# One core, two attention layers: where the norm weight and the gate enter the first one, and the size of one row sum

## The chip, the core and the metric

The kernel runs on one core of a Trainium2 chip. The core has five engines that run side by side, each with its own in-order queue: TensorE (PE in the profile; its weight loads stand apart as PEld), VectorE (DVE), ScalarE (ACT), GpSimd (POOL) and SyncE (SP), which here only issues DMAs. The metric is the device time of one execution in microseconds; a median over runs is compared with a median.

## What is computed

The reference is one inference step of a two-layer streaming encoder, in float32. 2048 new frames of one stream ("prompt") and 64 frames of a running stream ("sample", with 256 cached frames) go through both layers; width 1024, 4 heads of width 256. The layer that the change touches is the first one, differential attention:

```python
s = einsum('bqhmd,bkhmd->bhmqk', q, k) * DIFF_DH ** -0.5      # two maps m = 0, 1 per head
p = softmax(where(visible, s, NEG_INF))                        # block-causal mask, chunks of 64
w = p[:, :, 0] - lam * p[:, :, 1]                              # learned scalar lam
o = w @ v                                                      # 256 wide per head
o = rmsnorm(o, subln_w) * (1 - lam_init)                       # norm over the head's 256 values
o = o * silu(g)                                                # g: the gate, a projection of the input
y = x + o @ w_out
```

The second layer is stick-breaking attention (a running sum along each row in place of the softmax). A final RMSNorm follows, and the keys and values of both layers are outputs too.

## The kernel before

Everything is held transposed, with features on the 128 partitions and frames along the free axis. A float32 product is made of three matmuls: each operand is split into a rounded high half and a low rest (`split`, line 51 to 54: ScalarE copies the high half, VectorE or GpSimd subtracts), and `mm3` (lines 57 to 62) issues low x high, high x low and high x high.

The stages follow one another: the first layer's projections (`p_phase`, 0 to about 770 us in the profile), the first attention (`a_phase` with `layer == 0`, about 770 to 1314 us), the output projection (`o_phase`), the second layer's projections (`p_strassen`), the second attention (`a_phase` with `layer == 1`, about 2240 to 2735 us) and the last output projection with the final norm.

`do_g` in `p_phase` makes the gate: it evaluates silu in seven steps on VectorE and ScalarE and writes the result to a scratch tensor `gT` in HBM, from which the attention reads it back.

In `a_phase` the work of one head is cut into five query groups: one of the 64 sample frames (against 320 keys) and four of 512 prompt frames (against 512, 1024, 1536 and 2048 keys). A group has four rows of 128 queries. For a row, `diff_unit` makes two maps: per 512 keys TensorE fills a PSUM tile `s`, and VectorE moves it to SBUF and takes its maximum (line 727); ScalarE takes the exponential of each whole map (line 735); VectorE computes the weight of the second map (lines 738 and 739) and adds the second map, times that weight, to the first in one instruction as long as the row (line 742). Row lengths run from 128 to 2048 columns.

With four rows done, the group's product with the values runs key block by key block: `transposed` turns the four 128 x 128 pieces of a block into one PSUM tile `tp` (line 791), splits it into `wh` and `wl`, and `pv_block` adds six matmuls into the two PSUM tiles `o`. There are only two `o` tiles, so the next group's first product has to wait until both have been read.

`mixed` ends a group. It issues the load of the gate `g` (one buffer per width), reads both `o` tiles with ScalarE twice, once squared into `sq` (line 827) and once times the norm weight into `ot` (line 829, or 840 for the last group; one `ot` buffer per width), and GpSimd adds the squares up. `finish`, called one key block into the next group, sums the squares over the partitions by a matmul with ones (line 844), makes the norm factor, multiplies `ot` by it (line 859, by VectorE at line 857 for the last group) and by the gate (line 860), and stores `ot`.

The order in each queue is not the order of the program text alone: a planner (`schedule_with_timeline_sim=True`) orders the instructions at build time by its own estimate of when each can start, and places the semaphores. The generators interleave the stages: matmuls of the next row and row operations of the previous one are drawn in turn by their `yield` costs, and the rows run ahead of the products by `LEAD` units.

Of the kernel before, what the change touches and what calls it, by code (L numbers as in the profile page):

```python
# [8 lines left out]
F32 = mybir.dt.float32  # L9
# [3 lines left out]
AF = mybir.ActivationFunctionType  # L13
ALU = mybir.AluOpType
# [3 lines left out]
P = 128  # L18
# [10 lines left out]
LAM_INIT = 0.8 - 0.6 * math.exp(0.0)  # L29
# [65 lines left out]
def p_phase(tc, k, layer, xsrc, rs):  # L95
# [4 lines left out]
    nc = tc.nc  # L100
    with ExitStack() as es:
# [160 lines left out]
        def do_g(h, wt, ti, ps0=None):  # L262
            t0, w = TT[ti]
            for s in range(2):
                ps = ps0 if s == 0 and ps0 is not None else proj_t(wt, s * P, ti)
                e, o = work("t1" if s else "t2", bufs=1)[:, :w], work("o1" if s else "o2")[:, :w]
                nc.vector.scalar_tensor_tensor(o, ps, -0.5, rbc[ti], ALU.mult, ALU.mult)
                r = op.tile([P, 2, 256], F32R, tag="s2", name="r", bufs=2).rearrange("p a b -> p (a b)")
                r = r[:, :w].bitcast(F32)
                nc.scalar.activation(e, o, AF.Exp, scale=-1.0)  # L270
                nc.vector.tensor_scalar(e, e, 1.0, 1e37, ALU.add, ALU.min)
                nc.scalar.activation(r, e, AF.Ln)
                nc.scalar.activation(r, r, AF.Exp, scale=-1.0)
                nc.vector.tensor_tensor(e, e, r, ALU.mult)
                nc.vector.scalar_tensor_tensor(o, o, -1.0, r, ALU.mult, ALU.mult)
                nc.vector.scalar_tensor_tensor(o, e, -2.0, o, ALU.add, ALU.mult)
                r0 = h * HW + s * P
                nc.sync.dma_start(out=k.gT[layer][r0:r0 + P, t0:t0 + w], in_=o)
# [14 lines left out]
        with pool(tc, f"prep{layer}") as pk:  # L293
            first, stat = prep(order[0], pk)
            st = [stat]
# [333 lines left out]
def a_phase(tc, k, layer):  # L629
    nc = tc.nc  # L630
    ck, cv = k.ckT[layer], k.cv[layer]
    with ExitStack() as es:
# [12 lines left out]
        if layer == 0:  # L645
            wk = es.enter_context(pool(tc, f"aw{layer}", 1))
        psp = es.enter_context(pool(tc, f"aps{layer}", 2, space=PSUM))
        osc = None
        if layer == 0:
            osc = wk.tile([P, 2], F32, name="osc")  # L650
            nc.scalar.activation(osc, k.subln_w, AF.Copy, scale=-0.5 * (1.0 - LAM_INIT))

        def pair(pl, tag, shape, bufs=None):
            t = pl.tile([P, 2] + shape, F32R, tag=tag, name=tag, bufs=bufs)
# [57 lines left out]
        def diff_unit(row, j, nq, qt, chunks, diag, s15):  # L712

            nk = sum(w for _, w, _ in chunks)
            nch = len(chunks)
            qs = slice(j * P, j * P + nq)
            st = wk.tile([P, 16], F32, tag="st", name="st", bufs=16)[:nq]
            r2 = rbp.tile([P, 2052], F32, tag="rb", name="r2")
            sc = float(P) ** -0.5
            maps = (row, r2)  # L720

            def matmuls():
                for m in range(2):
                    for ci, (kt, w, wn) in enumerate(chunks):
                        ps = psp.tile([P, 512], F32, tag="s", name="s", bufs=3)
                        s_matmul(ps, nq, wn, qt, qs, kt, [m], diag if ci == nch - 1 else None, w)
                        nc.vector.tensor_scalar(maps[m][:nq, ci * 512:ci * 512 + w], ps[:nq, :w], 1.0, None,  # L727
                                                ALU.mult, ALU.max, accum_out=st[:, 4 * m + ci:4 * m + ci + 1])
                        yield w / 2048
                    mx = st[:, 4 * m:4 * m + nch]  # L730
                    nc.vector.tensor_scalar(mx, mx, -sc, None, ALU.mult, ALU.min, accum_out=st[:, 8 + m:9 + m])

            def rowops():
                for m in range(2):
                    nc.scalar.activation(maps[m][:nq, :nk], maps[m][:nq, :nk], AF.Exp, scale=sc,
                                         bias=st[:, 8 + m:9 + m], accum_out=st[:, 10 + 2 * m:11 + 2 * m])
                    yield nk / 4096
                nc.vector.reciprocal(st[:, 14:15], st[:, 12:13])
                nc.vector.scalar_tensor_tensor(st[:, 14:15], st[:, 14:15], k.nlam[:nq], st[:, 10:11],
                                               ALU.mult, ALU.mult)  # L740
                nc.scalar.activation(s15[:nq, j:j + 1], st[:, 10:11], AF.Square, scale=(EPS * HW) ** 0.5)
                nc.vector.scalar_tensor_tensor(row[:nq, :nk], r2[:nq, :nk], st[:, 14:15], row[:nq, :nk],
                                               ALU.mult, ALU.add)
                yield nk / 2048

            return matmuls(), rowops()

# [69 lines left out]
        def mixed(u):  # L817

            h, wq, nq, t0 = u.h, u.wq, u.nq, u.t0
            oa, ob = u.o  # L820
            g = (gp if wq == 512 else wk).tile([P, 2, wq], F32, tag=f"g{wq}", name="g")
            nc.sync.dma_start(out=g, in_=rows(k.gT[layer], h, t0, t0 + wq))
            ot = wk.tile([P, 2, wq], F32, tag=f"ot{wq}", name="ot")
            if layer == 0:
                sq = wk.tile([P, 2, wq], F32, tag=f"sq{wq}", name="sq")
                for e, o in ((0, oa), (1, ob)):
                    nc.scalar.activation(sq[:, e, :wq], o[:, :wq], AF.Square)
                    if not u.last:
                        nc.scalar.activation(ot[:, e, :wq], o[:, :wq], AF.Copy, scale=osc[:, e:e + 1])
                nj = len(u.rows)  # L830
                dg = wk.tile([P, wq], F32, tag=f"rm{wq}", name="dg")
                nc.gpsimd.tensor_tensor(dg[:nq].rearrange("p (j q) -> p j q", j=nj),
                                        k.idn[:nq, :nq].unsqueeze(1).to_broadcast([nq, nj, nq]),
                                        u.s15[:nq, :nj].unsqueeze(2).to_broadcast([nq, nj, nq]), ALU.mult)
                (nc.vector if u.last else nc.gpsimd).tensor_tensor(sq[:nq, 0, :wq], sq[:nq, 0, :wq], dg[:nq], ALU.add)
                (nc.vector if u.last else nc.gpsimd).tensor_tensor(sq[:, 0, :wq], sq[:, 0, :wq], sq[:, 1, :wq],
                                                                   ALU.add)
                if u.last:
                    for e, o in ((0, oa), (1, ob)):
                        nc.scalar.activation(ot[:, e, :wq], o[:, :wq], AF.Copy, scale=osc[:, e:e + 1])  # L840

                def finish():
                    ss = psp.tile([P, 512], F32, tag="t", name="ss", bufs=3)[:, :wq]
                    nc.tensor.matmul(ss, k.ones, sq[:, 0, :wq], start=True, stop=True)
                    r = wk.tile([P, wq], F32, tag=f"rs{wq}", name="rs")
                    m = wk.tile([P, wq], F32, tag=f"rm{wq}", name="rm")
                    t = sq[:, 1, :wq]
                    nc.scalar.activation(m, ss, AF.Copy, scale=1.0 / HW)
                    nc.scalar.activation(r, m, AF.Ln)
                    nc.scalar.activation(r, r, AF.Exp, scale=-0.5)  # L850
                    nc.scalar.activation(t, r, AF.Square)
                    nc.gpsimd.tensor_tensor(t, t, m, ALU.mult)
                    nc.vector.tensor_scalar(t, t, -3.0, None, ALU.add)
                    nc.gpsimd.tensor_tensor(r, t, r, ALU.mult)
                    for e in range(2):
                        if u.last:
                            nc.vector.tensor_tensor(ot[:, e, :wq], ot[:, e, :wq], r, ALU.mult)
                        else:
                            nc.gpsimd.tensor_tensor(ot[:, e, :wq], ot[:, e, :wq], r, ALU.mult)
                        nc.gpsimd.tensor_tensor(ot[:, e, :wq], ot[:, e, :wq], g[:, e, :wq], ALU.mult)  # L860
                    nc.sync.dma_start(out=rows(k.oT[layer], h, t0, t0 + wq), in_=ot[:, :, :wq])

                unfinished.append(finish)
            else:
                for e, o in ((0, oa), (1, ob)):
                    nc.vector.tensor_tensor(ot[:, e, :wq], o[:, :wq], g[:, e, :wq], ALU.mult)
                nc.sync.dma_start(out=rows(k.oT[layer], h, t0, t0 + wq), in_=ot[:, :, :wq])
# [217 lines left out]
def trunk(ctx: ExitStack, tc, xT, wqkg, wv, wo, small, ckT, cv, rope, masks, idn,  # L1085
          yT, kT, v):
    nc = tc.nc
    k = K()
# [43 lines left out]
    k.y1T = dp.tile([D, T], F32, name="y1T")  # L1132
    k.xop = [dp.tile([7, P, 4, PW], F32, name=f"xop{i}") for i in range(2)]
    k.xs = dp.tile([P, NC, NS], F32, name="xs")
    k.wnm = cp.tile([P, NC], F32, name="wnm")
    nc.vector.tensor_scalar(k.wnm, k.norm_w[:, 1], -0.5, None, ALU.mult)

# [91 lines left out]
```

## Time and profile before

| | before |
|---|---|
| median of 3 runs | 2928.25 us (2926.78 to 2929.58) |
| the profiled execution's own time | 2934.8 us |
| its span, first to last instruction | 2933.0 us |
| TensorE busy | 2809.2 us, 96% of the span |
| VectorE busy | 1905.4 us, 65% |
| ScalarE busy | 1444.3 us, 49% |
| GpSimd busy | 572.4 us, 20% |
| mean granted TensorE clock | 0.984 of full speed |

The profile is one execution, taken instruction by instruction. A busy share is an average over stages that are limited in different ways, so a change in one stage is read from that stage's windows, waits and timeline. A wait is put down to the instruction whose end released it last.

### The profile page before, as it was taken

What the parts mean: (1) busy time and instruction counts of PE and PEld (TensorE: products, weight loads), DVE (VectorE), ACT (ScalarE), POOL (GpSimd) and SP (SyncE); (2) the same over time, 40 slices, a digit from 0 to 9 for tenths busy, and PEclk for the clock granted to TensorE, in tenths of its full rate; (3) what the DMA queues carried; (4) which work ended last, traced back from release to release, by engine and by line L of the source; (5) the groups of instructions that cost most, each with busy time, mean ns of one, the idle gap of its engine ahead of it and who ended that gap; (6) DMA issues with size and microseconds to landing.
All of it is one profiled execution on the core that took longest, in us unless ns stands there. A gap on an engine that the chain in (4) does not pass through costs nothing.

```text
span 2933.0 us, 45474 instructions
## 1 busy us (share of the span) xinstructions
PE 2809.2 (96%) x16342; PEld 2446.4 (83%) x16342; DVE 1905.4 (65%) x3586; ACT 1444.3 (49%) x2763; POOL 572.4 (20%) x639
## 2 busy tenths in 40 slices
PE   8999999999899999989989999999997999999998
PEld 7888998988787777768777987899996788788788
DVE  7644514345378887854556688765686988877455
ACT  6512322313466666653234444543455877776433
POOL 1233233231233544443000000000000000000321
PEclk9999999999999999999999999999998999999999
DMA  5577456354715443336754677765727334523442
GB/s 175 166 195 189 138 156 179 132 147 128 269 62 185 139 137 121 115 101 210 248 178 154 223 238 244 253 201 166 241 97 239 137 123 156 175 76 104 162 143 98
DMA packets 365938, 484.01 MB, mean 165 GB/s; under 512 B 63504, under 2 KB 208144, under 8 KB 365712
## 3 DMA queue, kind: packets, MB, share of 16 engines
q1 hardware_dynamic: 350560, 466.67, 49.8%
q10 hardware_dynamic: 15152, 14.44, 1.5%
q8 instruction: 129, 2.11, 0.3%
q14 instruction: 97, 0.79, 0.1%
HBM read 273.10 MB, written 207.88 MB: 164 GB/s over the span
## 4 chain that ended last, share of the span: by engine, by line
PE 67%; DVE 15%; DMA 8%; ACT 6%; issue 3%; POOL 1%; SPq 0%; ACTq 0%; DVEq 0%; POOLq 0%
PE pj L58 13%; PE pj L62 13%; PE pj L61 13%; DVE rowA L775 4%; PE ps L58 3%; PE ps L62 3%; PE ps L61 3%; PE o L58 3%; PE o L62 3%; PE o L61 3%; PE tp L791 2%; DVE rowA L772 2%; PE s L58 2%; PE s L62 2%; PE s L61 2%
## 5 line engine op out<-in xcount | busy, mean ns | idle before, releaser
L58 PE MATMUL pj<-x,wop 128*128 128x272 f32 (+1 forms) x1008 | 330.7, 330 | 26.1 <-DVE x L54 21.0
L58 PE MATMUL pj<-hl,whi 128*128 128x512 f32 (+2 forms) x960 | 340.3, 355 | 3.2 <-ACT whi L53 3.2
L61 PE MATMUL pj<-hh,wlo 128*128 128x512 f32 (+2 forms) x960 | 338.9, 353 | 1.0 <-POOL wlo L54 1.0
L62 PE MATMUL pj<-hh,whi 128*128 128x512 f32 (+2 forms) x960 | 338.6, 353 | 0.0
L62 PE MATMUL pj<-x,wop 128*128 128x272 f32 (+1 forms) x1008 | 328.5, 327 | 0.0
L61 PE MATMUL pj<-x,wop 128*128 128x272 f32 (+1 forms) x1008 | 328.2, 326 | 0.0
L58 PE MATMUL s<-k,q 128*128 128x512 f32 (+3 forms) x656 | 266.5, 407 | 23.9 <-DVE rowA L727 6.9
L58 PE MATMUL o<-wl,v 128*128 128x512 f32 (+4 forms) x688 | 270.4, 393 | 15.6 <-DVE wl L54 9.4
L62 PE MATMUL o<-wh,v 128*128 128x512 f32 (+4 forms) x688 | 250.7, 365 | 0.0
L61 PE MATMUL o<-wh,v 128*128 128x512 f32 (+4 forms) x688 | 249.8, 363 | 0.0
L54 DVE TENSOR_TENSOR wl<-tp,wh 128x512 fp32r<-128x512 f32 (+5 forms) x344 | 195.1, 576 | 83.7 <-ACT wh L53 83.2
L53 ACT ACTIVATE s<-o 128x256 fp32r<-128x256 f32 (+2 forms) x212 | 84.2, 404 | 333.2 <-DMA kS<-s 127.0
L61 PE MATMUL s<-k,q 128*128 128x512 f32 (+3 forms) x656 | 241.2, 368 | 0.0
L62 PE MATMUL s<-k,q 128*128 128x512 f32 (+3 forms) x656 | 241.2, 368 | 0.0
L58 PEld LDWEIGHTS pj<-x,wop 128*128 128x128 f32 x1008 | 191.1, 190 | 52.9 <-DVE x L54 30.2
L58 PE MATMUL ps<-ol,wh 128*128 128x512 f32 (+2 forms) x640 | 227.3, 355 | 6.2 <-DVE ol L54 6.2
L756 POOL MEMSET z<- 128x1 f32 (+1 forms) x68 | 12.0, 177 | 1123.9 <-PE pj L62 777.3
L61 PE MATMUL ps<-oh,wl 128*128 128x512 f32 (+2 forms) x640 | 229.4, 358 | 0.0
L53 ACT ACTIVATE wh<-tp 128x512 fp32r<-128x512 f32 (+5 forms) x344 | 169.5, 507 | 119.8 <-PE tp L791 106.2
L62 PE MATMUL ps<-oh,wh 128*128 128x512 f32 (+2 forms) x640 | 227.1, 355 | 0.0
L58 PEld LDWEIGHTS pj<-hl,whi 128*128 128x128 f32 x960 | 182.0, 190 | 26.9 <-ACT whi L53 3.5
L61 PEld LDWEIGHTS pj<-x,wop 128*128 128x128 f32 x1008 | 191.9, 190 | 14.7 <-DVE wop L54 0.6
(231 smaller groups left out, 7354.3 us busy)
## 6 DMA issues: line engine op xcount, KB each, us to landing
wraw<-in_wqkg SPq DMA_DIRECT2D x144, 256.0 KB, 3.9
vS<-s SPq DMA_DIRECT2D x128, 256.0 KB, 3.4
v<-vS SPq DMA_DIRECT2D x64, 512.0 KB, 5.2
q<-qS SPq DMA_DIRECT2D x60, 512.0 KB, 6.0
k<-kS SPq DMA_DIRECT2D x60, 512.0 KB, 7.3
wraw<-in_wv SPq DMA_DIRECT2D x64, 256.0 KB, 3.5
qS<-s SPq DMA_DIRECT2D x128, 128.0 KB, 2.4
kS<-s SPq DMA_DIRECT2D x128, 128.0 KB, 2.4
```

What stands on the lines that cost most here:

```text
L53: nc.scalar.activation(hi, x, AF.Copy)
L54: lo_eng.tensor_tensor(lo, x, hi.bitcast(F32), ALU.subtract)
L58: first = nc.tensor.matmul(ps, lh, rl, start=start, stop=False, skip_group_check=True)
L61: nc.tensor.matmul(ps, ll, rh, start=False, stop=False, skip_group_check=True)
L62: nc.tensor.matmul(ps, lh, rh, start=False, stop=stop, skip_group_check=True)
L756: nc.gpsimd.memset(z[:nq, nk:nk + 1], 0.0)
L772: nc.vector.scalar_tensor_tensor(rr, zz, 0.0, rr, ALU.min, ALU.subtract)
L775: nc.vector.tensor_tensor_scan(rv, z[:nq, c1:c0:-1], rv, r[:nq, c1:c1 + 1] if done else 0.0, ALU.add, ALU.subtract)
L791: nc.tensor.transpose(tp[:kn, j * P:j * P + u.nq], u.rows[j][:u.nq, i * P:i * P + kn], k.idn[:u.nq, :u.nq])
```

## The change

Three edits. The norm weight times 0.5 x (1 - lambda_init), which ScalarE applied as it read `o`, becomes a per-partition factor `k.nosc` in the gate's second last step (its sign is folded in: the gate was multiplied by -1.0 there). The product of `o` with the gate, which GpSimd made at the very end of `finish`, is made by VectorE straight from PSUM in place of ScalarE's scaled copy. And the sum of the two maps (line 742) is issued in pieces of at most 1024 columns, with a yield after each.

```diff
-                nc.vector.scalar_tensor_tensor(o, o, -1.0, r, ALU.mult, ALU.mult)
+                nc.vector.scalar_tensor_tensor(o, o, -1.0 if layer else k.nosc[:, s:s + 1], r, ALU.mult, ALU.mult)
...
-        osc = None
-        if layer == 0:
-            osc = wk.tile([P, 2], F32, name="osc")
-            nc.scalar.activation(osc, k.subln_w, AF.Copy, scale=-0.5 * (1.0 - LAM_INIT))
...
-                nc.vector.scalar_tensor_tensor(row[:nq, :nk], r2[:nq, :nk], st[:, 14:15], row[:nq, :nk],
-                                               ALU.mult, ALU.add)
-                yield nk / 2048
+                for c0, c1 in pieces(nk):
+                    nc.vector.scalar_tensor_tensor(row[:nq, c0:c1], r2[:nq, c0:c1], st[:, 14:15], row[:nq, c0:c1],
+                                                   ALU.mult, ALU.add)
+                    yield (c1 - c0) / 2048
...
                     if not u.last:
-                        nc.scalar.activation(ot[:, e, :wq], o[:, :wq], AF.Copy, scale=osc[:, e:e + 1])
+                        nc.vector.tensor_tensor(ot[:, e, :wq], o[:, :wq], g[:, e, :wq], ALU.mult)
...
                 if u.last:
                     for e, o in ((0, oa), (1, ob)):
-                        nc.scalar.activation(ot[:, e, :wq], o[:, :wq], AF.Copy, scale=osc[:, e:e + 1])
+                        nc.vector.tensor_tensor(ot[:, e, :wq], o[:, :wq], g[:, e, :wq], ALU.mult)
...
-                        nc.gpsimd.tensor_tensor(ot[:, e, :wq], ot[:, e, :wq], g[:, e, :wq], ALU.mult)
...
+    k.nosc = cp.tile([P, 2], F32, name="nosc")
+    nc.vector.tensor_scalar(k.nosc, k.subln_w, 0.5 * (1.0 - LAM_INIT), None, ALU.mult)
```

`pieces(nk)` cuts 0 to nk into steps of 1024. It was there before, for the second layer.

## Rows read from the trace of the kernel before

**Rows 1.** The page's first part: busy time of an engine, share of the span, instructions.

```profile
PE 2809.2 (96%) x16342; PEld 2446.4 (83%) x16342; DVE 1905.4 (65%) x3586; ACT 1444.3 (49%) x2763; POOL 572.4 (20%) x639
```

**Rows 2.** Busy time by stretch of the span. Columns: the stretch in us, its length, busy us (and instructions) of PE, PEld, DVE, ACT and POOL, the granted TensorE clock, the DMA share and GB/s. The first stretch lies in the first layer's projections; the others in the first attention: most of it, the first 25 us of two heads, and the end.

```profile
250.00:500.00 250.00, 250.00 (x1495) 226.32 (x1494) 102.02 (x169) 67.57 (x150) 83.63 (x88) 1.00 0.58 161
...
803.00:1276.00 473.00, 457.22 (x2484) 370.08 (x2484) 380.74 (x1191) 298.01 (x603) 196.91 (x198) 1.00 0.37 123
...
950.00:975.00 25.00, 23.15 (x122) 18.40 (x121) 23.05 (x68) 17.77 (x29) 16.39 (x17) 1.00 0.27 89
...
1200.00:1225.00 25.00, 22.70 (x125) 18.04 (x124) 21.31 (x65) 17.37 (x35) 15.21 (x19) 1.00 0.28 88
...
1275.00:1300.00 25.00, 18.79 (x83) 14.86 (x84) 14.83 (x18) 14.79 (x28) 17.48 (x12) 0.80 0.33 104
```

**Rows 3.** What TensorE waited for in the first attention (803 to 1314 us): the waiting instruction, its releaser, us in total, times, the longest.

```profile
PE tp L791 <- DVE rowA L742: 8.0, 4, 4.1
PE s L58 <- DVE rowA L727: 5.2, 4, 2.7
PE o L58 <- DVE wl L54: 3.3, 2, 3.0
PE ss L844 <- DVE sq L836: 2.3, 1, 2.3
PE s L58 <- DMA k<-kS: 2.2, 1, 2.2
PE s L58 <- DVE r L727: 1.6, 1, 1.6
...
PE ss L844 <- POOL sq L836: 0.9, 2, 0.7
```

**Rows 4.** Single waits of TensorE in that stage, from its timeline. Columns: start, duration, engine, line, instruction, shape, count of like neighbours, and in brackets the idle time before it and its releaser.

```profile
882.00 0.55 PE L791 MATMUL tp<-idn,rowA 128*128 128x128 f32 x3 [1.14 <-DVE rowA L742]
...
892.72 0.55 PE L791 MATMUL tp<-idn,rowA 128*128 128x128 f32 x3 [1.41 <-DVE rowA L742]
...
963.71 0.50 PE L58 MATMUL s<-k,q 128*128 128x512 f32 x1 [1.74 <-DVE rowA L727]
...
1278.16 0.90 PE L791 MATMUL tp<-idn,rowA 128*128 128x128 f32 x3 [4.07 <-DVE rowA L742]
...
1282.11 0.80 PE L58 MATMUL o<-wl,v 128*128 128x512 f32 x1 [3.05 <-DVE wl L54]
```

**Rows 5.** The start of the kernel, from the timelines of TensorE and ScalarE: the first matmul, and ScalarE writing the fourth quarter of the weight tile `whi` that this matmul reads from.

```profile
5.66 0.77 PE L58 MATMUL pj<-wlo,hh 128*128 128x256 f32 x2 [5.66 <-ACT hh L150]
...
10.83 0.63 ACT L53 ACTIVATE whi<-wraw 128x512 fp32r<-128x512 f32 x1 [1.19 <-DMA wraw<-in_wv]
```

**Rows 6.** Groups of instructions by line and shape. Columns: line, engine, operation, tiles, out shape <- in shape, count, busy us, mean ns of one, idle time before them. Lines 829, 860 and 742 in the first attention, 772, 775 and 866 in the second.

```profile
L829 ACT ACTIVATE ot<-o,osc 128x512 f32<-128x512 f32 x30 | 19.9, 690 | 1.0 <-DMA oT<-ot 1.0
...
L860 POOL TENSOR_TENSOR ot<-ot,g 128x512 f32<-128x512 f32 x30 | 44.0, 1482 | 0.0
...
L742 DVE SCALAR_TENSOR_TENSOR rowA<-r,st,rowA 128x2048 f32<-128x2048 f32 x4 | 9.4, 2346 | 0.0
...
L772 DVE SCALAR_TENSOR_TENSOR rowA<-z,rowA 128x1024 f32<-128x1024 f32 x40 | 48.6, 1216 | 16.5 <-ACT rowA L771 16.3
...
L775 DVE TENSOR_TENSOR_SCAN rowA<-z,rowA 128x1024 f32<-128x1024 f32 x40 | 94.2, 2354 | 0.3
...
L866 DVE TENSOR_TENSOR ot<-o,g 128x512 f32<-128x512 f32 x32 | 21.2, 680 | 1.4 <-PE o L62 1.2
...
L866 DVE TENSOR_TENSOR ot<-o,g 128x64 f32<-128x64 f32 x8 | 1.4, 209 | 0.0
```

**Rows 7.** The end of the first attention, from the timelines of VectorE and ScalarE (same columns as rows 4).

```profile
1275.76 2.35 DVE L742 SCALAR_TENSOR_TENSOR rowA<-r,st,rowA 128x2048 f32<-128x2048 f32 x1
1278.03 3.43 DVE L54 TENSOR_TENSOR ol<-oraw,oh 128x512 fp32r<-128x512 f32 x2
1281.38 1.87 DVE L54 TENSOR_TENSOR wl<-tp,wh 128x512 fp32r<-128x512 f32 x3
...
1311.66 0.68 ACT L840 ACTIVATE ot<-o,osc 128x512 f32<-128x512 f32 x1
```

**Rows 8.** The start of the second head, from the timelines of GpSimd, VectorE and ScalarE.

```profile
960.27 3.22 POOL L860 TENSOR_TENSOR ot<-ot,g 128x512 f32<-128x512 f32 x3
...
960.93 2.11 DVE L742 SCALAR_TENSOR_TENSOR rowA<-r,st,rowA 128x1408 f32<-128x1408 f32 x1
...
955.84 1.07 ACT L827 ACTIVATE sq<-o 128x512 f32<-128x512 f32 x2
...
966.39 1.25 ACT L829 ACTIVATE ot<-o,osc 128x512 f32<-128x512 f32 x2
```

**Rows 9.** Waits that bear on the moved product: SyncE's queue in the first attention, and TensorE in the second (the same columns as rows 3).

```profile
SPq L861 <- POOL ot L860: 224.7, 18, 25.1
...
PE o L58 <- DVE ot L866: 4.8, 4, 1.8
```

**Rows 10.** The gate's step and an instruction of the same kind with a per-partition factor, both in the first projections (columns as rows 6), and the constant beside which the new one is made (min/median/max ns, first and last start in us).

```profile
L275 DVE SCALAR_TENSOR_TENSOR o<-o,r 128x512 f32<-128x512 f32 x24 | 17.5, 730 | 0.0
...
L151 DVE SCALAR_TENSOR_TENSOR hl<-x,vecs,hh 128x512 fp32r<-128x512 f32 x24 | 18.4, 772 | 9.3 <-ACT hh L150 9.3
...
L1136 DVE TENSOR_SCALAR wnm<-vecs x1: 173/173/173, 4.3 to 4.3; 128x8 f32<-128x8 f32 x1
```

## The prediction

> **What bounds the kernel now.** I read the page's busy times first: TensorE is busy for 96% of the span, VectorE for 65% [rows 1]. So the change can shorten the kernel only where TensorE waits. The windows come next, cut at the stage that the change touches: from 803 to 1276 us TensorE is busy 457.2 of 473.0 us and VectorE 380.7, or 80% [rows 2]. VectorE is the second fullest engine there, and in the first 25 us of the second head it is as busy as TensorE, 23.05 against 23.15 us. Third, the waits: those of TensorE that are listed come to 23.5 us, and all but 3.1 have VectorE as releaser [rows 3]. ScalarE releases none. This is the purse: the change cannot give much more than that, and a microsecond saved on ScalarE or GpSimd is worth something only through VectorE's queue.
>
> The timeline shows where those waits lie [rows 4]. Four are transposes that wait for a sum of the two maps (8.0 us with the one of 1.4 that is left of the total [rows 3]). The largest pair stands at the end of the stage: 4.07 us for the last sum, then 3.05 us for `wl`, and the granted clock of that stretch is 0.80 [rows 2], so matmuls after the pause also run longer. Others are matmuls of `s` whose PSUM tile VectorE has not emptied yet, because a long sum stands ahead in its queue.
>
> **Part 1, the weight folded into the gate.** 40 instructions of the first projections get a per-partition factor in place of a constant. A like instruction with such a factor takes 772 ns, the present one 730 [rows 10]; both means hold some that ran long. At worst 40 x 0.04 = 1.7 us more on VectorE, and what hides it is TensorE, busy 250.00 of 250.00 us there with VectorE at 102 [rows 2]. Cost 0; were that cover gone, 1.7. The constant is one more instruction like the 173 ns one at 4.3 us [rows 10]: 0, at most 0.2. The dropped `osc` was one short ScalarE instruction: 0.
>
> **Part 2, o times gate on VectorE.** ScalarE loses 40 copies, the 512-wide at 690 ns, GpSimd loses 40 products, the 512-wide at 1482 ns [rows 6]. VectorE gains 32 products of 680 ns and 8 of 209, priced by the same instruction in the second attention [rows 6]: 21.8 + 1.7 = 23.5 us, which takes its share of the stage from 80% to about 85%.
>
> What is queued behind the new instruction on VectorE are the emptying of `s`, the `wl` halves and the sums, all of which TensorE waits for. Its own waits could be three. *The gate*: its buffer is now free as soon as the product is made, a whole group ahead, and in the second attention, where the same load stands in front of the same product, VectorE idles 1.2 us for `o` and nothing for the gate [rows 6]: cost 0. *The `ot` buffer*: it is free when the previous group's store has read it. The store stands in SyncE's queue behind GpSimd's gate product, 224.7 us of waiting in 18 [rows 9]; it now follows the product before that one and goes 2 x 1.5 us sooner [rows 6]. Cost 0; if it is still late, VectorE and not ScalarE is held, and the 1.0 us that ScalarE waited [rows 6] is the bound. *Two readers of one `o` tile*: if ScalarE's square and VectorE's product had to take turns, that would be the present sequence on one engine, so no worse.
>
> *The release of `o`.* In the second head ScalarE squares at 955.84 but copies only at 966.39 [rows 8]: the `ot` buffer is held by a late `finish`, and the next group's products wait with it. TensorE fills the time with `s` matmuls, which is what crowds VectorE. The new order frees `o` some microseconds sooner. Against that, the second attention shows what the moved product can cost: TensorE waits 4.8 us in 4 places for it [rows 9], there behind scans of 2.35 us [rows 6]. Here the longest will be the pieces, 1.22. I take a loss of 1.0 us, between 0 (now, with ScalarE) and 4.8.
>
> *The start of each head*, where VectorE is full. Against: a 64-wide and a 512-wide pair, 0.4 + 1.2 us, come into a stretch with 1.95 us of VectorE left [rows 2]; half of it on the path in three heads is 2.4 us. For: the 1408-wide sum took 2.11 us while GpSimd made gate products, and TensorE waited 1.74 us behind it [rows 4, 8]; a like wait of 1.6 stands in the list [rows 3]. In two pieces, and with the gate product gone from GpSimd, each of these loses about 0.9: 1.8. And the ones-matmul waits 0.9 us for squares that stood behind gate products on GpSimd [rows 3]: 0.9. Net gain 0.3, between a loss of 4.4 and a gain of 4.4 (all the waits there).
>
> *The last group*: of the 2.3 us wait before its ones-matmul [rows 3], ScalarE's copy between the two squares (0.68) [rows 7] goes. Gain 0.4; if the planner puts both products ahead of the additions on VectorE, a loss of 1.0.
>
> **Part 3, the sum in pieces.** Rows over 1024 columns: 8 in each of 4 heads, so 32 instructions more. Two of 1024 cost 2 x 1216 = 2432 ns against 2346 for one of 2048 [rows 6], 0.09 each, 2.8 us in all on VectorE. A fifth on the path: 0.5, between 0 and 2.8. [...]
>
> What the pieces buy: the transposes of the first eight key blocks need only the first piece, 1.13 us sooner (2.35 - 1.22). That needs dependences by region and not by tile. The start of the trace shows these: the first matmul runs at 5.66 us, and ScalarE still writes another quarter of its weight tile at 10.83 [rows 5]. At the three waits outside the end, of 1.14, 1.41 and 1.4 us [rows 3, 4], that is 1.14 + 1.13 + 1.13 = 3.4; part goes into the next wait (`wl`), so I take 2.4, between 0 and 4.0.
>
> At the end of the stage: the last sum at 1275.76, then two `ol` halves of the next stage for 3.43 us, then `wl` [rows 7]. If VectorE's order stays, TensorE resumes at the same time and nothing is won. But `wl` becomes ready about a microsecond sooner, so that I expect one `ol` to fall behind it: 1.7 us. Bounds 0 and 5.9 (both `ol` behind, 3.3, and some 2.6 for 13 matmuls of 0.63 that would take 0.4 at full clock).
>
> **The sum**, against the profiled execution (span 2933.0, own time 2934.8): gains 2.4 + 1.7 + 0.4 + 0.3 = 4.8, losses 1.0 + 0.5 = 1.5, so about 3.3 us, to 2931.5. That execution stands 6.6 us above the median of the runs; on the median the forecast is 2928.25 - 3.4, rounded: 2924.8. A difference within 0.2% (5.9 us) is about what a measurement of this kernel cannot tell from no change.
>
> **The rivals.**
> *More is won (30%).* The three sums give 3.4, the end 5, the starts of the heads 3, and the moved product costs nothing: about 11 us, 2917. For it: all these waits have one releaser, whose long instructions are cut. Against: VectorE's 23.5 us more.
> *VectorE becomes the bound at the heads' starts (17%).* If the 1.6 us added there meet no slack in four heads (6.4), and the second attention's 4.8 us of waiting for the product appears here, less the 3.4 us of the sums: 7.8 us slower, 2936. It decides where VectorE's busy time in such 25 us passes about 24; it is at 23.05 in the second head and 21.31 in the fourth [rows 2]. [...]
> *The pieces release nothing early (8%).* If transposes wait for both pieces, 2.4 and 1.7 go: 0.8 us slower, 2929.
>
> **How the numbers follow.** The forecast has 45%, the rivals 30, 17 and 8. All of the forecast's and the third rival's chance lies within 0.2%; of the first rival's I leave nearly all below, of the second's about 13 points above. With the planner free to reorder whatever comes later, I round to faster 0.32, same 0.53, slower 0.15. The range 2915 to 2935 takes in two thirds of the first rival and half of the second; the forecast alone is 2922.5 to 2927.5.
>
> **What would show it.** Right: no transposes waiting over 0.5 us on line 742's sum outside the end, the pause at the end under 6 us, the product by VectorE at 0.68 us a piece with no wait for the gate, `ot` in the second head made within 6 us of the squares, GpSimd over 40 us emptier. Wrong: TensorE waiting for `ot`, VectorE at over 24 of 25 us at the heads' starts, or `wl` still behind two `ol` at the end. A time outside the range would mean that the planner's new order moved waits that I hold fixed, in this stage or a later one.

## The result, and the profile after

The changed kernel takes 2959.82 us (median of 4 runs, 2958.14 to 2967.95) beside 2928.91 us for the one before: 1.0106 times as long, 95% interval 1.0087 to 1.0124, some 31 us slower. The forecast was 2924.8 us and the range ended at 2935. The profiled execution spans 2966.2 us, 33.2 more than before.

The engines' busy times, from the page of the changed kernel:

```profile
PE 2826.2 (95%) x16342; PEld 2455.2 (83%) x16342; DVE 1940.7 (65%) x3659; ACT 1428.6 (48%) x2722; POOL 523.4 (18%) x599
```

Work moved as foretold: VectorE 35.3 us up, GpSimd 49.0 down, ScalarE 15.7 down [rows 1]. TensorE has the same matmuls and is still busy 17 us longer, so they ran slower. Its windows say when (columns as in rows 2; the first line is of the kernel before, the others of the changed one):

```profile
803.00:1311.00 508.00, 487.01 (x2629) 394.38 (x2630) 398.99 (x1213) 315.79 (x635) 216.94 (x213) 0.99 0.37 122
...
803.00:1335.00 532.00, 497.83 (x2628) 399.97 (x2626) 429.94 (x1281) 299.44 (x597) 171.93 (x175) 0.97 0.35 116
950.00:975.00 25.00, 24.29 (x127) 19.13 (x127) 23.62 (x60) 16.30 (x33) 14.86 (x18) 1.00 0.27 87
1025.00:1050.00 25.00, 21.65 (x110) 17.39 (x109) 20.09 (x81) 16.06 (x42) 6.34 (x6) 0.86 0.73 258
```

The stretch from 1025 to 1050 us, with a mean granted clock of 0.86 (0.50 from 1029 to 1035 us and 1.00 from 1036 us on, in windows of 1 us), has no counterpart before (1.00 from 1025 to 1050 us). The last `o` product of the first attention comes at 1335.1 us in place of 1310.9, though the first came at the same time (806.8 and 807.3). So 24 of the 33 us arise in the stage that was changed. The first two windows, which end with that product, divide them: TensorE is busy 11 us longer, at a granted clock of 0.97 in place of 0.99, and idle 13 us longer. Another 6 arise in the second attention, where no instruction was changed: its gate products run from 2252.3 to 2729.0 us before and from 2278.4 to 2761.1 after.

TensorE's waits from 803 to 1345 us (engine, tile, line, releaser; total, times, longest):

```profile
PE s L58 <- DVE rowA L723: 12.9, 12, 2.7
PE tp L788 <- DVE rowA L739: 7.7, 6, 5.0
PE s L58 <- DMA k<-kS: 5.4, 2, 3.3
PE o L58 <- DVE wl L54: 4.4, 2, 3.1
PE s L58 <- DVE r L723: 4.4, 7, 1.3
PE ss L841 <- DVE sq L833: 3.0, 1, 3.0
PE tp L788 <- DVE wl L54: 1.2, 1, 1.2
PE ss L841 <- POOL sq L833: 0.6, 1, 0.6
```

39.6 us in place of about 25 [rows 3]. What grew most is not the wait for the sum (line 739 now) but the emptying of `s` (line 723): 17.3 us against 6.8; the wait for a load of `k` grew too, 5.4 against 2.2. The sums themselves went from 95.9 us of VectorE's time (68 instructions) to 116.6 (100). The timelines of VectorE, GpSimd and ScalarE at 1015 us, the end of the second head, show one reason (the last two lines are VectorE and ScalarE in the kernel before):

```profile
1014.76 4.49 DVE L739 SCALAR_TENSOR_TENSOR rowA<-r,st,rowA 128x1024 f32<-128x1024 f32 x2
...
1028.62 2.52 DVE L739 SCALAR_TENSOR_TENSOR rowA<-r,st,rowA 128x1024 f32<-128x1024 f32 x2
...
1016.17 2.13 POOL L833 TENSOR_TENSOR sq<-sq 128x512 f32<-128x512 f32 x1
1018.26 2.11 POOL L54 TENSOR_TENSOR k<-raw,k 128x512 fp32r<-128x512 f32 x1
...
1014.12 1.09 ACT L824 ACTIVATE sq<-o 128x512 f32<-128x512 f32 x2
...
1015.26 2.34 DVE L742 SCALAR_TENSOR_TENSOR rowA<-r,st,rowA 128x2048 f32<-128x2048 f32 x1
...
1017.16 0.60 ACT L827 ACTIVATE sq<-o 128x512 f32<-128x512 f32 x1 [2.12 <-PE o L62]
```

A row of 1920 columns in two pieces takes 4.49 us where GpSimd works, and GpSimd's own instructions take 2.1; where GpSimd is all but idle (0.57 us busy from 1028 to 1032 us), the two pieces of a longer row (2048) take 2.52. A second reason shows in the same rows. The head's last sum starts at 1028.62, 14.5 us after ScalarE squared the previous group at 1014.12. Before, it started at 1015.26, 1.9 us ahead of that square at 1017.16. So the order of the work is another one.

### The profile page after: what moved, and what is told of

Read it like the earlier page. It is cut to its first block, busy times and chain, and to the rows that moved or that the text cites. A ratio compares the mean times of both kernels' runs of the same rounds, so it can differ in the third digit from the quotient of the medians.

```text
span 2966.2 us, 45473 instructions
## 1 busy us (share of the span) xinstructions
PE 2826.2 (95%) x16342; PEld 2455.2 (83%) x16342; DVE 1940.7 (65%) x3659; ACT 1428.6 (48%) x2722; POOL 523.4 (18%) x599
## 3 DMA queue, kind: packets, MB, share of 16 engines
q8 instruction: 129, 2.11, 0.3%
## 4 chain that ended last, share of the span: by engine, by line
PE 65%; DVE 16%; DMA 8%; ACT 6%; issue 3%; POOL 0%; SPq 0%; ACTq 0%; DVEq 0%; POOLq 0%
PE pj L58 12%; PE pj L61 12%; PE pj L62 12%; DVE rowA L772 4%; PE ps L61 3%; PE ps L58 3%; PE ps L62 3%; PE o L58 3%; PE o L62 3%; PE o L61 3%; PE s L58 2%; PE tp L788 2%; PE s L62 2%; PE s L61 2%; DVE rowA L769 2%
## 5 line engine op out<-in xcount | busy, mean ns | idle before, releaser
L58 PE MATMUL s<-k,q 128*128 128x512 f32 (+3 forms) x656 | 272.3, 416 | 37.4 <-DVE rowA L723 15.6
L61 PE MATMUL s<-k,q 128*128 128x512 f32 (+3 forms) x656 | 244.6, 373 | 0.0
L62 PE MATMUL s<-k,q 128*128 128x512 f32 (+3 forms) x656 | 244.5, 373 | 0.0
L58 PEld LDWEIGHTS pj<-x,wop 128*128 128x128 f32 x1008 | 192.0, 191 | 53.1 <-DVE x L54 26.1
L61 PEld LDWEIGHTS pj<-x,wop 128*128 128x128 f32 x1008 | 193.0, 191 | 14.4 <-DVE wop L54 0.4
L62 PEld LDWEIGHTS pj<-x,wop 128*128 128x128 f32 x1008 | 192.3, 191 | 15.1
```

The lines of the kernel that those rows point to most:

```text
L58: first = nc.tensor.matmul(ps, lh, rl, start=start, stop=False, skip_group_check=True)
L61: nc.tensor.matmul(ps, ll, rh, start=False, stop=False, skip_group_check=True)
L62: nc.tensor.matmul(ps, lh, rh, start=False, stop=stop, skip_group_check=True)
```

## The experiments

Three theories. A: a cut sum costs, because VectorE and GpSimd take turns. B: the product that VectorE took over costs. C: the planner writes another order of all queues after any edit, and that costs. Ratios are to runs of the kernel before on the same chip; microseconds are the ratio's excess times 2930. "Clock" is the mean over a kernel's runs of span x (1 - mean granted clock), what TensorE lacked to full clock; for the kernel before it is 46 to 50 us, chip by chip, and for the changed kernel 61. It is not lost time one for one: among the 70 runs of the kernel before, a run with one microsecond more in this column is only 0.2 to 0.5 us longer (a straight line through the runs of each chip).

| run | work | order of the queues | ratio (95%) | us | clock |
|---|---|---|---|---|---|
| changed kernel | all three edits | new | 1.0106 (1.0087 to 1.0124) | +31 | 61.4 |
| e1_pieces | pieces | new | 1.0063 (1.0040 to 1.0086) | +18 | 58.2 |
| e2_product | fold, product | new | 1.0059 (1.0038 to 1.0080) | +17 | 57.2 |
| e3_fold | fold | new | 1.0042 (1.0029 to 1.0056) | +12 | 53.7 |
| p1_pieces | pieces | as before | 1.0044 (1.0029 to 1.0059) | +13 | 57.4 |
| p2_product | fold, product | as before | 1.0029 (1.0018 to 1.0041) | +8 | 53.4 |
| p3_fold | fold | as before | 1.0008 (0.9995 to 1.0021) | +2 | 50.2 |
| p_all | all three edits | as before | 1.0053 (1.0033 to 1.0072) | +16 | 55.2 |
| l15_before | none (`LEAD` 15) | new | 1.0033 (1.0020 to 1.0046) | +10 | 54.1 |
| l18_after | all three (`LEAD` 18) | new | 1.0117 (1.0102 to 1.0132) | +34 | 60.8 |
| q0_quiet | GpSimd products out | as before | 0.9989 (0.9977 to 1.0000) | -3 | 52.4 |
| q1_quiet_pieces | the same, and pieces | as before | 0.9993 (0.9983 to 1.0004) | -2 | 49.2 |
| v_ol | two `ol` moved | as before but for them | 0.9999 (0.9989 to 1.0009) | 0 | 46.2 |
| v_end | two `ol` moved, last sum cut | as before but for them | 1.0010 (1.0000 to 1.0021) | +3 | 46.1 |

### Each part alone

e1_pieces is before with the third edit, e2_product the changed kernel without it. e3_fold has the first edit alone; it keeps ScalarE's copy, without its factor, and GpSimd's gate product (one place of its edit against before):

```diff
...
-                        nc.scalar.activation(ot[:, e, :wq], o[:, :wq], AF.Copy, scale=osc[:, e:e + 1])
+                        nc.scalar.activation(ot[:, e, :wq], o[:, :wq], AF.Copy)
...
```

> Before with one part of the change: the sum of the two maps in pieces of 1024; ScalarE's copy of o and GpSimd's gate product stay. Theory A (the cut sum is what costs: beside GpSimd's work a pair of pieces holds VectorE some 1 to 2 us longer than one whole sum, 20.7 us of VectorE time in all in the changed kernel's trace): slower by 15 to 25 us, the sum's busy time up by at least 15 us over its 95.9 us before. Theory B (the product that VectorE takes over costs, 23.5 us of its time): within 4 us of before. Theory C (any edit makes the planner write another order of matmuls, with S rows less far ahead in heads 2 to 4): whatever TensorE's order does; it decides if the order changes and the sum's busy time does not.

> The changed kernel with the sum of the two maps whole again: the weight is in the gate, and VectorE makes o times gate. Theory A (the cut sum costs): slower than before by 0 to 8 us at most, with the long sums near 2.35 us. Theory B (the product costs): slower by 20 to 30 us, and the last o product of the first attention 15 to 24 us later than before's 1310.9 us.

> Only the weight folded into the gate: ScalarE copies o without a factor, GpSimd multiplies by the gate as before, and the sum stays whole. No engine's work changes by more than 2 us, so theories A and B both expect it within 3 us of before. Theory C (the planner's new order after any edit is the cost): slower by 10 us or more with the same busy times.

All three lose 12 to 18 us, the control too, and 18 and 17 do not add up to 31 with a control of 12 in each. e1_pieces meets A's time, its sums at 110.7 us being 14.8 up where A asked for 15; e2_product lies between what A and B expected; e3_fold meets C. So C is part of it, and the parts cannot be read from kernels that the planner has reordered.

### The same edits in the order of before

The order that the planner gave the kernel before was written down, and every instruction was given an order dependence on the one ahead of it in its queue (an order of issue only; `out` is the queue):

```diff
...
+        for a, c in zip(out, out[1:]):
+            tc.add_manual_dep(c, a.name, mybir.DependencyInfo(mybir.DependencyClass.NoSync,
+                                                              mybir.DependencyReason.DATA), reason="order")
...
```

TensorE's order is then the same: counted from the traces by tile and shape, none of its 16342 places holds another matmul in these runs, against 2022 places in the changed kernel and 1788 in e3_fold.

> The weight folded into the gate alone, as in the run e3_fold, but with every engine's queue held to the order that the planner gave the kernel before (an order dependence from each instruction to the next on its engine). Theory C (e3_fold's 12 us came from the new order that the planner wrote, not from the edit): within 4 us of before. If the edit itself costs (a slower instruction, another engine's wait): 8 us or more slower, as e3_fold was.

> The sum in pieces of 1024 alone, every queue in the order of the kernel before, the second piece right behind the first. Theory A (a cut sum takes longer beside GpSimd, where VectorE and GpSimd alternate at each instruction): the sums' busy time rises by 8 to 20 us over 95.9, and the kernel is slower by 3 to 12 us. Theory C (order alone): within 4 us of before. If the early first piece is worth what the prediction took, 2 to 4 us faster.

> The weight folded and o times gate by VectorE, the sum whole; every queue in the order of the kernel before, each product put into VectorE's queue at the place where ScalarE's copy ran in the trace of before, and each load of a gate in SyncE's queue one place ahead of the store that stood before it. Theory B (23.5 us more on VectorE are what costs): 8 to 20 us slower. Theory C: within 4 us of before, with VectorE's busy time 15 to 25 us up.

> The whole change with every queue in the order of the kernel before (the product and the gate's load placed as in p2_product). Theory C: within 6 us of before, so that at least 25 of the change's 31 us are the planner's new order. Theories A and B: the sum of what p1_pieces and p2_product show, 10 us or more.

The fold costs nothing that can be told: C holds for e3_fold. The whole change costs 16 us in the old order and 31 in its own: half of the loss is the order, less than the 25 of 31 that C had asked for. In the old order the second attention also has its old length (gate products from 2259.5 to 2736.5 us in p_all, 477.0 against 476.7 before and 482.7 after). The pieces cost 13 us, a little over A's 3 to 12, and the product with the fold 8, B's lower end. Together that would be 21, the upper end of p_all's interval, so whether the parts simply add is not decided.

Why the pieces cost is seen at two places where the old order puts a cut sum beside GpSimd's products. First before, then p1_pieces, then q1_quiet_pieces (below), each the timeline of VectorE, with GpSimd's products where there are any (of a group of four, two are 64 wide):

```profile
1215.49 4.47 POOL L860 TENSOR_TENSOR ot<-ot,g 128x512 f32<-128x512 f32 x4
1216.15 2.11 DVE L742 SCALAR_TENSOR_TENSOR rowA<-r,st,rowA 128x1408 f32<-128x1408 f32 x1
1260.51 3.20 DVE L742 SCALAR_TENSOR_TENSOR rowA<-r,st,rowA 128x1920 f32<-128x1920 f32 x1
...
1260.42 4.43 POOL L860 TENSOR_TENSOR ot<-ot,g 128x512 f32<-128x512 f32 x2
```

```profile
1219.60 4.37 POOL L919 TENSOR_TENSOR ot<-ot,g 128x512 f32<-128x512 f32 x4
1220.28 3.23 DVE L798 SCALAR_TENSOR_TENSOR rowA<-r,st,rowA 128x1024 f32<-128x1024 f32 x2
1266.89 4.37 DVE L798 SCALAR_TENSOR_TENSOR rowA<-r,st,rowA 128x1024 f32<-128x1024 f32 x2
...
1266.80 3.52 POOL L919 TENSOR_TENSOR ot<-ot,g 128x512 f32<-128x512 f32 x2
```

```profile
1213.16 1.80 DVE L798 SCALAR_TENSOR_TENSOR rowA<-r,st,rowA 128x1024 f32<-128x1024 f32 x2
1255.49 2.35 DVE L798 SCALAR_TENSOR_TENSOR rowA<-r,st,rowA 128x1024 f32<-128x1024 f32 x2
```

Each cut adds 1.1 to 1.2 us while GpSimd multiplies. TensorE waits longer behind both in p1_pieces (its timeline; 1.62 and 0.29 us before), and in the 10 us that follow each pause the granted clock is 0.83 (windows, columns as in rows 2; the same two stretches of before, 1219 to 1229 and 1264 to 1274, have 1.00). This is one execution of each, and in the last section the same waits come with a lower clock in one execution and without it in another:

```profile
1224.18 0.63 PE L113 MATMUL s<-k,q 128*128 128x512 f32 x1 [2.71 <-DVE r L782]
...
1271.92 0.59 PE L113 MATMUL o<-wl,v 128*128 128x512 f32 x1 [1.81 <-DVE wl L109]
...
1224.00:1234.00 10.00, 9.82 (x38) 7.49 (x39) 7.19 (x25) 7.07 (x11) 1.36 (x2) 0.83 0.38 113
1271.00:1281.00 10.00, 9.08 (x38) 7.43 (x38) 6.63 (x20) 2.74 (x5) 0.41 (x2) 0.83 0.40 131
```

In p2_product VectorE stops for two things at places where ScalarE had made the copy: for the store that frees `ot` (3.10 us, with TensorE waiting 2.5 behind it), and it makes a product just ahead of the last sum, so that the long pause at the end is 5.2 us:

```profile
845.34 0.69 DVE L886 TENSOR_TENSOR ot<-o,g 128x512 f32<-128x512 f32 x1 [3.10 <-DMA oT<-ot]
...
1281.83 0.69 DVE L886 TENSOR_TENSOR ot<-o,g 128x512 f32<-128x512 f32 x1
1282.44 2.80 DVE L797 SCALAR_TENSOR_TENSOR rowA<-r,st,rowA 128x2048 f32<-128x2048 f32 x1
```

Both come from where the product was put, so 8 us is its price in this order, not in every one.

### The two engines by themselves

m1_port holds none of the attention, only sums and products (`row` = r2 x w + `row`) on VectorE, with and without a row of GpSimd products of 128x512.

> No attention at all, only VectorE's sum and product by themselves (the output is filler): 8 sums of 2048 and 8 pairs of 1024 first alone, then the same beside an unbroken row of GpSimd products of 128x512, then 16 products that read PSUM and 16 that read two SBUF tiles beside such a row. Theory A: alone a pair of pieces costs what a whole sum does within 0.2 us; beside GpSimd the whole sum keeps its 2.3 us or waits once, and a pair waits twice, so that it takes 0.5 us or more longer than the whole; GpSimd's products are made longer by the wait. The product from PSUM should not be made longer. If a pair costs the same as a whole sum beside GpSimd too, the cut is not dearer by contention, and A has to find its 20.7 us elsewhere.

Groups by form: sums alone (the first two lines) and beside GpSimd (two); then timelines of the two engines beside whole sums, beside pieces, and of GpSimd alone; then VectorE's products with one input in PSUM beside GpSimd, with both in SBUF beside GpSimd, and with both in SBUF alone:

```profile
L1105 DVE SCALAR_TENSOR_TENSOR row<-r,vec,row 128x1024 f32<-128x1024 f32 x16 | 19.2, 1279 | 0.0
L1105 DVE SCALAR_TENSOR_TENSOR row<-r,vec,row 128x2048 f32<-128x2048 f32 x8 | 18.7, 2336 | 0.2
...
L1105 DVE SCALAR_TENSOR_TENSOR row<-r,vec,row 128x2048 f32<-128x2048 f32 x8 | 26.1, 3260 | 0.3
L1105 DVE SCALAR_TENSOR_TENSOR row<-r,vec,row 128x1024 f32<-128x1024 f32 x8 | 17.3, 2165 | 0.3
...
49.93 9.73 POOL L1111 TENSOR_TENSOR pb<-pb,pa 128x512 f32<-128x512 f32 x3
52.04 9.77 DVE L1105 SCALAR_TENSOR_TENSOR row<-r,vec,row 128x2048 f32<-128x2048 f32 x3
...
78.24 6.57 DVE L1105 SCALAR_TENSOR_TENSOR row<-r,vec,row 128x1024 f32<-128x1024 f32 x3
79.40 6.52 POOL L1111 TENSOR_TENSOR pb<-pb,pa 128x512 f32<-128x512 f32 x3
...
93.08 1.26 POOL L1111 TENSOR_TENSOR pb<-pb,pa 128x512 f32<-128x512 f32 x1
...
L1126 DVE TENSOR_TENSOR row<-o,row 128x512 f32<-128x512 f32 x16 | 11.1, 691 | 1.0 <-DVE pb L1109 0.5
...
L1130 DVE TENSOR_TENSOR row<-r,row 128x512 f32<-128x512 f32 x16 | 22.4, 1398 | 0.6
...
L1114 DVE TENSOR_TENSOR row<-row,pb 128x512 f32<-128x512 f32 x4 | 2.8, 692 | 52.0 <-POOL pb L1111 51.9
```

Alone, eight rows cost 18.7 us whole and 19.2 cut, 0.06 a cut. Beside GpSimd a whole sum takes 3.26 us and a pair of pieces 2 x 2.165 = 4.33: 1.07 a cut, the figure of the kernel's own rows. In the timelines three sums and three products of GpSimd go by in the same 9.8 us, and three pieces and three products in 6.6. So in these rows the engines alternate at every instruction, and more instructions are more turns. VectorE's product with both inputs in SBUF doubles, 692 to 1398 ns; the one with an input in PSUM takes 691 beside GpSimd (680 in the second attention [rows 6]). A whole sum loses 0.92 us a turn (3.26 less 2.34) where GpSimd's product takes 1.26 alone; no run shows what it is that the engines take turns at.

### Without GpSimd's products

```diff
...
-                            nc.gpsimd.tensor_tensor(ot[:, e, :wq], ot[:, e, :wq], r, ALU.mult)
-                        nc.gpsimd.tensor_tensor(ot[:, e, :wq], ot[:, e, :wq], g[:, e, :wq], ALU.mult)
...
```

> Control for the next run: the kernel before in its own order, without the four GpSimd products of each group's end (o times the norm factor, and times the gate, are left out, so that the output lacks both). About 120 us less GpSimd work in the first attention. Expected within 5 us of before; if VectorE loses time to GpSimd there, up to 8 us faster, with the sums' busy time a few us below 95.9.

> p1_pieces (the sum in pieces, every queue in the order of before) without those four GpSimd products of each group. Theory A (the cut sum costs because VectorE and GpSimd alternate at each instruction): the difference to q0_quiet is at most half of the 13 us by which p1_pieces was slower than before, and a piece of 1024 takes 1.3 us or less on average in place of 1.45. If a cut sum costs by itself (the fixed cost of an instruction, other waits), the difference stays at 10 us or more.

The 13 us are gone: q1 is at 0.9993 and q0 at 0.9989, with overlapping intervals. A's first number holds. Its second does not: a piece takes 1343 ns on average, above the 1.3 us expected (1409 in p1_pieces), and the sums still total 101.1 us against 91.3 in q0_quiet. So VectorE's time for the cut fell only from 13.5 to 9.8 us; GpSimd still adds the squares there. TensorE's waits in the stage rise by 1.4 us with the cut, with GpSimd's products (25.0 to 26.4) and without them (20.5 to 21.9). What differs is the clock: cutting raises that column by 9 us or so with GpSimd's products there (57.4 against 48.7 for before on that chip) and not without them (49.2 against 52.4). In the profiled executions p1_pieces has TensorE busy 8.5 us longer than before (2817.7 against 2809.2) in a span that is 10.4 us longer, and q1_quiet_pieces has it busy no longer than q0_quiet (2806.1 against 2810.0). So the products of GpSimd are needed for the loss, and in these executions most of it is the same matmuls taking longer, at a mean granted clock of 0.980 in place of 0.984 (0.983 in q0_quiet, 0.985 in q1_quiet_pieces). The rows above show a lower clock behind such a sum at two places of one execution; that this accounts for all of the 13 us was not shown. q0_quiet also bounds what taking these products off GpSimd can win in this order: about 3 us.

### Another order, the same work

> The kernel before with LEAD = 15.0 in place of 16.0: no instruction is added, removed or made longer, but the planner writes another order (in TensorE's queue about as many places differ as in e3_fold). If the order of before is a favourable one among many (so that nearly any rewriting costs), 6 to 18 us slower, as e3_fold was. If e3_fold's loss has to do with its edit, within 4 us of before.

> The changed kernel with LEAD = 18.0: the same work in another order by the planner. If the half of the 31 us that p_all does not show is chance of the order, this lands elsewhere between p_all and the changed kernel, 5 to 15 us faster than the latter; if it belongs to what the edits make the planner believe, it stays within 5 us of the changed kernel's 2959.8.

l15_before has the edit `LEAD = 15.0` and no other; 10 us slower, with another matmul at 2143 places of TensorE's queue, shows that the order before was the better of these two. l18_after stays where the changed kernel is (34 us beside 31), so the loss is not one unlucky draw; that is two orders, and which of the planner's beliefs makes them so is open.

### The end of the stage

v_ol moves two `ol` halves behind the last group's first three `wl` in VectorE's queue; v_end cuts the last sum too.

> The kernel before in its own order, except that in VectorE's queue the two ol halves of the next stage that stood between the last sum and the last group's first wl stand behind that group's first three wl. The prediction's term for the end (1.7 us for one ol, bounds 0 and 5.9): the wait for wl of 3.05 us falls to 1.0 us or less, the o products resume 2 us sooner, and the kernel is 2 to 5 us faster, the upper part if the stretch of lowered clock behind the pause gets shorter. If the pause there is hidden by what follows: no difference.

> v_ol with, besides, the very last sum (head 4, the last row) alone in two pieces of 1024. If the first transposes start when the first piece is done: the pause at the last sum falls from 4.07 to about 3.0 us, and the kernel is 1 us faster than v_ol. Theory A (beside GpSimd's addition of 3.41 us there): the second piece takes 0.5 us or more longer, wl comes as much later, and the 1 us is given back, so that v_end equals v_ol within 1 us.

VectorE's timeline in v_ol, then TensorE's:

```profile
1280.49 1.89 DVE L116 TENSOR_TENSOR wl<-tp,wh 128x512 fp32r<-128x512 f32 x3 [1.37 <-ACT wh L115]
1282.29 1.69 DVE L116 TENSOR_TENSOR ol<-oraw,oh 128x512 fp32r<-128x512 f32 x2
...
1281.23 0.79 PE L120 MATMUL o<-wl,v 128*128 128x512 f32 x1 [1.51 <-DVE wl L116]
...
1293.19 0.50 PE L120 MATMUL o<-wl,v 128*128 128x512 f32 x1 [0.55 <-DVE wl L116]
```

The wait for `wl` falls from 3.05 to 1.51 us, as `wl` now waits for ScalarE's `wh`; 0.55 returns as a wait 12 us later, and the kernel is no faster; the 2 to 5 us that were expected did not come, though a single microsecond would not show in an interval of 3 us either way. In v_end:

```profile
1273.12 3.50 DVE L807 SCALAR_TENSOR_TENSOR rowA<-r,st,rowA 128x1024 f32<-128x1024 f32 x2
...
1274.46 0.79 PE L858 MATMUL tp<-idn,rowA 128*128 128x128 f32 x3 [3.00 <-DVE rowA L807]
1277.58 0.80 PE L121 MATMUL o<-wl,v 128*128 128x512 f32 x1 [2.33 <-DVE wl L117]
```

The transposes start 1.3 us after the first piece began, before the second is done, and their wait falls from 4.07 to 3.00 us, as expected. But the two pieces take 3.50 us, and the wait for `wl` is 2.33 in place of 1.51: theory A's trade. No version here that does the whole work beats the kernel before.

## Why the prediction was wrong, point by point

*What bounds the kernel* was right in part: TensorE's waits have VectorE as releaser, but the time that TensorE loses to a lower clock is no wait, and outside the end of the stage the working had no term for it. The clock column is up by 12 to 15 us in the changed kernel, and TensorE is busy 17 us longer. *The fold* was right: nothing in the old order. *VectorE's share of the product* was right: 20.3 + 1.4 + 1.3 = 23.0 us (line 826 and 837) for 23.5, no wait for the gate, `ot` of the second head at 961.0 and 962.2, within 6 us of its square at 956.7.

*The sum of all terms* failed first where it held the order fixed. The working allowed a new order in a closing remark and gave it no term; it is half of the loss, 31 - 16 us, the 6 of the second attention among them. An edit of `LEAD` alone costs 10 us, three times the forecast gain. Most of the signs of being right came about all the same (GpSimd 49 us emptier, the product at 0.68 us, one transpose outside the end waiting over 0.5 us for the sum), so they did not tell a gain from a loss.

*The cut priced at 0.09 us.* The row for the piece [rows 6] is of the second attention, where GpSimd is all but idle, 34.1 us in 500 (the fifth of the busy times):

```profile
2240.00:2740.00 500.00, 477.25 (x2574) 397.26 (x2573) 397.17 (x500) 359.73 (x629) 34.07 (x104) 0.98 0.40 133
```

Beside GpSimd it is 1.1, and the 2.8 us became 13.5 in p1_pieces and 20.7 in the changed kernel. The sign was in rows that the prediction quoted: the 1408-wide sum of 2.11 us beside gate products [rows 8], where 1408/2048 of 2346 ns is 1.61. The prediction saw GpSimd there, but took cutting for a part of the cure; by the rows of m1_port, where a whole sum takes 0.92 us longer beside GpSimd and a cut adds 1.07, the 0.5 us are time lost to GpSimd's turn, and a cut adds a turn.

*The early first piece* was right in mechanism. In p1_pieces the waits for the sum fall from 8.0 to 4.0 us, the transposes starting on the first piece, as v_end's rows show. (The row that it took for this from the kernel's start [rows 5] reads `wlo`, not the `whi` that is still being written; the next matmul, at 6.23 us, does read `whi`, so the reading stands.) But the wait for `wl` goes from 3.3 to 7.1 and all waits together from 25.0 to 26.4: `wl` stands in VectorE's queue behind the second piece.

*The end, 1.7 us*, was wrong in size and did not come about: in the changed kernel both `ol` still stand ahead of `wl`, the pause is 4.98 + 3.05 us against 4.07 + 3.05 [rows 4], and v_ol, which brings it about, is no faster. *The last group* went the way of its bound: the product stands between the additions, 3.0 us for 2.3.

*The product, 1.0 us* was too low for the old order (8 with the fold); the store wait of 3.10 us that p2_product shows is the one whose bound was put at 1.0. *The rival that ends slower* had the sign but not the place: VectorE stays at 23.62 of 25 us in the second head's start, under its limit of 24, and the two largest new waits for VectorE, 2.73 us each for it to empty `s` (at 1020.5 and 1293.5 us), are among the long rows of the second and fourth heads. *Small sums*: the waits at the heads' starts come to 4.2 us, not 4.4, and 13 matmuls at 0.63 in place of 0.4 to 3.0, not 2.6; neither bears on the outcome.

## What to carry to other kernels

Where a planner orders the queues, compare an edit with its neighbour in the same order (pin it) before giving the time to the edit; a control that changes next to no work cost 10 to 12 us here. Price a VectorE instruction with two SBUF inputs from rows that run beside GpSimd (692 ns alone and 1398 beside it in m1_port), and count the cuts as turns (1.07 us each there). A result released early is worth something only if what the consumer needs next does not stand behind the rest of the same work.

## What was not expected of the hardware

The granted clock was not fixed by the program. The kernel before ran 70 times, on four chips, with a mean granted clock of 0.980 to 0.987 and in 2925 to 2944 us. p3_fold and before have the same order of matmuls and the same list of waits, 24.3 and 25.0 us in all, and p3_fold runs 2 us earlier at this place; yet from 887 to 897 us p3_fold ran at 0.66 with TensorE busy for 7.94 us, and before, from 889 to 899, at 1.00 with 7.79 (p3_fold first):

```profile
887.00:897.00 10.00, 7.94 (x26) 5.46 (x27) 8.79 (x34) 5.54 (x21) 2.37 (x1) 0.66 1.04 378
...
889.00:899.00 10.00, 7.79 (x38) 5.75 (x39) 9.50 (x38) 5.94 (x23) 0.29 (x1) 1.00 1.02 361
```

So a lower clock in one stretch of one execution is weak evidence, and the clock of a kernel is compared over several runs. And GpSimd loses with VectorE: in m1_port its product takes 1.26 us alone, three take 6.52 beside pieces and three 9.73 beside whole sums.
